# Decay masking, decay products and a convolution tap change engines in a two-layer hybrid trunk

## The chip, the cores and the metric

The kernel runs on one core of one Trainium2 chip. The metric is device time in microseconds (us) of one execution. Before the change the median of three runs is 2238.65 us, the lowest 2234.93 us and the highest 2241.45 us.

Engines are called PE (TensorE, matrix products), PEld (TensorE's weight loads), DVE (VectorE), ACT (ScalarE), POOL (GpSimd) and SP (SyncE, which issues most transfers).

## The reference, cut to what matters

Two layers of a transformer trunk over 512 latent tokens, with a context of 256 tokens before them; the width is 1024, everything is float32. Per layer, for context and latents with the same weights:

```
h   = rmsnorm(x) * (1 + scale) + shift
qkv, z, a, b, c_q, c_kv, k_rope = split(h @ w_in)
u   = silu(conv5(qkv))                     # short convolution over time, 5 taps, per column
q,k = l2norm(u_q), l2norm(u_k);  v = u_v
g   = -exp(a_log) * softplus(a + dt_bias); beta = sigmoid(b)
# gated delta rule in chunks of 64, in both directions of time, latents start from the context's state
gc    = cumsum(g)
decay = exp(where(i >= j, gc_i - gc_j, -inf))
A     = where(i > j, (k*beta) k^T * decay, 0);   solve (A + I) against v*beta and k*beta*exp(gc)
qk    = q k^T * decay;   qg = q * exp(gc)
scan over chunks: S, o
y   = concat(rmsnorm(o)*silu(z), latent_attention(...)) @ w_out
x  += gate1 * y;   x += gate2 * swiglu(modulated rmsnorm(x))
```

In the second layer the context is only needed for keys, values and the final state. At the end there is one rmsnorm.

## The kernel before, in words

All activations lie transposed, with 128 feature rows on the partitions and tokens along the free dimension. A large product is made of three products in a reduced float32 form: each operand is split into a high and a low part, `hi = copy(x)` on ACT and `lo = x - hi` on DVE (lines 205, 206, 210 to 212), and PE adds hi*hi, hi*lo and lo*hi (`gemm`, lines 214 to 222). Weights are split in the same way just ahead of their use, 512 columns at a time (`load_w`), so that PE, in its order, waits for ACT and DVE at each weight tile.

The work is written as generators, the streams: `ctx_in`, `ctx_mla`, `ctx_ffn`, `ctx_in1` once, and `ctx_chain`, `mod_rest`, `lat_in`, `lat_chain`, `mla_prep`, `mla_att`, `lat_ffn` for each layer (lines 1152 to 1313). After each step a stream yields three planned costs: how long the step takes until its successor can follow, the PE time and the DVE time in it. `weave` (lines 78 to 102) is the planner: it keeps a planned clock for PE and for DVE and a due time for each stream, and always writes out the next step of the stream that can start first on PE's planned clock; between equals the rank decides. The pair in `TUNE` (lines 51 to 70) is a stream's rank and a factor on its costs: a smaller factor brings a stream's steps closer together. Some steps wait for a name that another stream reports as done (`need`). The order of writing is a priority; the order on each engine can differ from it where an operand is late.

The delta rule's streams (`ctx_chain`, `lat_chain`) go through `gdn_pre` and `gdn_scan`. `gdn_pre` is run six times: for the context and for two halves of the latents' heads in layer 0, for the context and the two halves in layer 1. It works on tiles of 128 partitions by 16 units of 64 columns (128x1024). For each direction d it takes the broadcast cumulated decay `gb[d]`, which comes by a transfer on POOL's queue; if queries are wanted (five of six times) ACT writes `qg[d] = exp(gb[d])` (line 516); POOL masks `gb[d]` in place, in two halves of 64 partitions, with `affine_select` and the fill -1e30 (lines 517 to 520); DVE subtracts a column (line 523), and ACT takes exp (line 524). Then PE makes k k^T and q k^T and DVE multiplies them by the decay (lines 540 to 551). POOL multiplies `qg[d]` by q (line 555), fills four tiles (lines 558 to 561), and DVE solves the triangular systems in 31 steps of two small operations (lines 571 to 576). PE, ACT and DVE finish with products of 64x64 blocks. `gdn_scan` goes over the chunks in order of time.

`conv` (lines 433 to 443) takes a projected chunk in PSUM: POOL clears two columns at each edge of `raw`, ACT copies the chunk into its middle, DVE makes tap 0 as a product with a scalar (line 440) and adds taps 1 to 4 (line 442), and `silu2` ends it. A latent chunk is 128x512, a context chunk 128x256. There are 24 latent chunks (12 per layer) and 20 context chunks (12 and 8).

Of the kernel before, what the change touches and what calls it, by code (L numbers as in the profile page):

```python
# [14 lines left out]
AF = mybir.ActivationFunctionType  # L15
ALU = mybir.AluOpType
# [4 lines left out]
P = 128  # L21
# [11 lines left out]
SLOT = 776  # L33

C_ID, C_BLK1, C_TRIF, C_TRIB, C_SEL, C_MSK, C_ONE, C_BLKM, C_QB = 0, 128, 256, 384, 512, 520, 524, 525, 527
NCONST = 529
B_MOD, N1, N2, CW, AL, DT, GN, QN, KN, FN = 0, 48, 56, 64, 124, 132, 140, 141, 143, 144
NSMALL = 152

# [9 lines left out]


TUNE = {
    ("ctx_in", 0): (3, 0.749),
    ("ctx_mla", 0): (3, 0.7),
    ("ctx_ffn", 0): (3, 1.003),
    ("ctx_in1", 0): (2, 1.0),
    ("ctx_chain", 0): (0, 1.0),
    ("mod_rest", 0): (1, 0.7),
    ("lat_in", 0): (2, 0.595),
    ("lat_chain", 0): (1, 1.0),
    ("mla_prep", 0): (4, 1.064),  # L60
    ("mla_att", 0): (5, 0.374),
    ("lat_ffn", 0): (6, 1.0),
    ("ctx_chain", 1): (2, 0.85),
    ("mod_rest", 1): (1, 1.0),
    ("lat_in", 1): (1, 1.0),
    ("lat_chain", 1): (0, 0.6),
    ("mla_prep", 1): (5, 1.755),
    ("mla_att", 1): (5, 1.07),
# [37 lines left out]
def trunk_kernel(ctx, tc, xin, cc, wmod, small, win, wuq, wuk, wuv, wout, wgu, wdn, cst, rope, out):  # L106
    nc = tc.nc
    V, A, G, PE = nc.vector, nc.scalar, nc.gpsimd, nc.tensor
# [18 lines left out]
    def slot(tag, dt=F32, w=None):  # L127
        width = WIDTH[tag]
        t = sp.tile([P, width], dt, name=nm(tag), tag=tag, bufs=BUFS[tag])
        return t[:, 0:w or width]  # L130
# [4 lines left out]
    def sm(shape, tag, dt=F32, bufs=1):  # L135
        return mp.tile(shape, dt, name=nm(tag), tag=tag, bufs=bufs)

    def tt(out, a, b, op=ALU.mult, e=None):
        (e or V).tensor_tensor(out=out, in0=a, in1=b, op=op)  # L139

    def ts(out, a, s1, s2=None, op0=ALU.mult, op1=ALU.add, e=None):
        if s2 is None:
            (e or V).tensor_scalar(out=out, in0=a, scalar1=s1, scalar2=None, op0=op0)
        else:
            (e or V).tensor_scalar(out=out, in0=a, scalar1=s1, scalar2=s2, op0=op0, op1=op1)

    def stt(out, a, s, b, op0, op1):
        V.scalar_tensor_tensor(out=out, in0=a, scalar=s, in1=b, op0=op0, op1=op1)  # L148

    def act(out, a, f, **kw):  # L150
        A.activation(out, a, f, **kw)  # L151

    def cpy(out, a):
        act(out, a, AF.Copy)
# [4 lines left out]
    nc.sync.dma_start(out=cct, in_=cc)  # L159
    cst_t = cp.tile([P, NCONST], F32, name="cst")  # L160
    nc.sync.dma_start(out=cst_t, in_=cst)
# [267 lines left out]
    def silu2(dst, src, th):  # L429
        act(th, src, AF.Tanh, scale=0.5)  # L430
        stt(dst, th, 1.0, src, ADD, MUL)

    def conv(l, st, p, chunk, dst):
        n = st.n
        raw = slot(st.t, w=n + 4)
        G.memset(raw[:, 0:2], 0.0)
        G.memset(raw[:, n + 2:n + 4], 0.0)
        cpy(raw[:, 2:n + 2], p)
        cw = smalls[l][:, CW + 5 * chunk:CW + 5 * chunk + 5]
        ts(dst, raw[:, 0:n], cw[:, 0:1])  # L440
        for j in range(1, 5):
            stt(dst, raw[:, j:j + n], cw[:, j:j + 1], dst, MUL, ADD)
        silu2(dst, dst, raw[:, 0:n])

# [3 lines left out]
    def u3(t):  # L448
        return t.rearrange("p (c i) -> p c i", i=64)

    U = 16

    def gdn_pre(l, st, hjs, kf, qf, vf, gt, res):
# [6 lines left out]
        def col(t, d):  # L460
            return t[:, u0(d):u0(d) + U]

        full = qf is not None
        gb = [slot("g4") for _ in range(2)]
        kt = slot("g4")
        qg = [slot("g4") for _ in range(2)] if full else []
# [47 lines left out]
        for d in range(2):  # L514
            if full:
                act(qg[d], gb[d], AF.Exp)
            for hp in range(2):
                s = slice(64 * hp, 64 * hp + 64)
                G.affine_select(out=u3(gb[d])[s], in_=u3(gb[d])[s], compare_op=ALU.is_ge, fill=-1e30, base=0,
                                pattern=[[0, U], [1 if d == 0 else -1, 64]], channel_multiplier=-1 if d == 0 else 1)  # L520
            dc = sm([P, U], "dc")
            tt(dc, col(gcb, d), lw, ADD)
            tt(u3(gb[d]), u3(gb[d]), dc.unsqueeze(2).to_broadcast([P, U, 64]), SUB)
            act(gb[d], gb[d], AF.Exp)
            kw = sm([P, U], "kw", bufs=4)
            tt(kw, col(ekl, d), rw)
            kws.append(kw)
            yield 4, 0, 1.6
# [11 lines left out]
        for b in range(0, U, nb):  # L540
            pt = ps("B")
            pv = pt.rearrange("p (c z i) -> p c z i", z=nz, i=64)
            for c in range(nb):
                for z, f in enumerate((kf, qf)[0:nz]):
                    for hp in range(2):
                        s = slice(64 * hp, 64 * hp + 64)
# [5 lines left out]
            yield 3, 1, 1.6  # L552
        if qf is not None:
            for d in range(2):
                tt(qg[d], qf, qg[d], e=G)
        bm = gb
        bd, L, M = (slot("g4") for _ in range(3))
        G.memset(bd[:, 0:1], 0.0)
# [12 lines left out]
        for r in range(31):  # L571
            n, m = 31 - r, r + 1
# [39 lines left out]
        for dst, lh, rh in ((us, vv, (vs, vs)), (W, ke, vv)):  # L612
            for a in range(0, U, 4):
                pt = ps("B")
                pv = pt.rearrange("p (n d i) -> p n d i", d=2, i=64)
                for q in range(4):
                    n, hi = divmod(a + q, nh)
                    for d in range(2):
                        c = hi * nch + (nch - 1 - n if d else n)
                        for hp in range(2):  # L620
                            s = slice(64 * hp, 64 * hp + 64)
# [187 lines left out]
    scale = 96.0 ** -0.5  # L809
# [249 lines left out]
    class Mix:  # L1059
# [21 lines left out]
        def use(self, m, p):  # L1081
            l, st = self.l, self.st
            kind, hj = m
            if kind == "tail":
                ab = slot("m" if st is CTX else "ox", w=st.n)
                cpy(ab, p)
                self.kr = ab
                self.gates = gates(l, st, ab)
            elif kind in "kqv":
                g = [g for g in self.gset if hj in g][0]  # L1090
                f = self.f[g]
                i = g.index(hj)
                ch = {"q": 0, "k": 4, "v": 8}[kind] + hj
                if g in self.spilled:
                    if kind not in f:
                        f[kind] = dp.tile([len(g), P, st.n], F32, name=nm("fscr"), tag=nm("fscr"))
                    t = slot(st.t, w=st.n)
                    conv(l, st, p, ch, t)
                    nc.gpsimd.dma_start(out=f[kind][i], in_=t)
                else:  # L1100
                    if kind not in f:
                        f[kind] = slot("g4")
                    conv(l, st, p, ch, f[kind][:, st.n * i:st.n * i + st.n])
            elif kind == "z":
                self.z[hj] = self.part("z", hj)
                silu2(self.z[hj], p, slot(st.t, w=st.n))
            else:
                t = slot("m" if st is CTX else "hd", w=st.n)
                cpy(t, p)
                if kind == "ckv":  # L1110
                    self.ckv = t
                else:
                    self.cq.append(t)

        def stage(self, g):
            f = self.f[g]
            if g in self.spilled:
                for kind in "kqv":
                    t = slot("g4")
                    nc.sync.dma_start(out=t.rearrange("p (j t) -> p j t", j=len(g)), in_=f[kind].rearrange("j p t -> p j t"))  # L1120
                    f[kind] = t
            return gdn_pre(self.l, self.st, g, f["k"], f.get("q"), f["v"], self.gates, self.pre[g])
# [237 lines left out]
def _constants():  # L1360
    f = np.float32
    c = np.zeros((P, NCONST), f)
    p = np.arange(P)
    c[:, C_ID:C_ID + P] = np.eye(P, dtype=f)
    c[:, C_ONE] = 1.0 / D
    same = (p[:, None] // 64) == (p[None, :] // 64)
    c[:, C_BLKM] = (p < 64) / 64.0
    c[:, C_BLKM + 1] = (p >= 64) / 64.0
    c[:, C_BLK1:C_BLK1 + P] = same
    c[:, C_QB] = 64 * EPS * (p < 64)  # L1370
    c[:, C_QB + 1] = 64 * EPS * (p >= 64)
    c[:, C_TRIF:C_TRIF + P] = same & (p[:, None] <= p[None, :])
    c[:, C_TRIB:C_TRIB + P] = same & (p[:, None] >= p[None, :])
    for j in range(4):
        for r in range(2):
            c[32 * j + r, C_SEL + 2 * j + r] = 1.0
    first = (p // 32) % 2 == 0
    c[:, C_MSK] = first
    c[:, C_MSK + 1] = ~first
    c[:, C_MSK + 2] = -1.0 * first  # L1380
    c[:, C_MSK + 3] = -1.0 * ~first
    t = np.arange(NL)
    inv = f(10000.0) ** (-np.arange(0, 16, 2, dtype=f) / f(16))
    ang = []
    for pos in ((t // GRID_W).astype(f), (t % GRID_W).astype(f)):
        a = pos[:, None] * inv[None, :].astype(f)
        ang += [a, a]
    ang = np.concatenate(ang, axis=1).astype(f)
    sign = np.where((np.arange(32) % 16) < 8, -1.0, 1.0).astype(f)
    rope = np.concatenate([np.tile(np.cos(ang).T.astype(f), (4, 1)), np.tile(np.sin(ang).T * sign[:, None], (4, 1))], axis=1)  # L1390
    return c, rope
# [57 lines left out]
```

## Time and profile before

| | |
|---|---|
| median of 3 runs | 2238.65 us |
| the profiled execution: its time | 2228.82 us |
| its span, first to last instruction | 2227.0 us |
| PE busy | 2034.1 us, 91% |
| DVE busy | 1497.3 us, 67% |
| ACT busy | 871.5 us, 39% |
| POOL busy | 127.1 us, 6% |
| rate of all transfers in the first of 40 slices | 319 GB/s |
| mean granted clock of PE | 0.946 of full speed |

The busy time of an engine is the union of its instructions. PE's instructions are pipelined and their ends are modelled, so that a PE busy all the time can still be fed late. An idle time in brackets stands behind the instruction that ended it, with the engine and line that released it. In a row of stretches the numbers are the length, then each engine's busy time and (with an x) its instructions, PE's granted clock, the busy share of the transfer engines, and GB/s.

### The profile page before, as it was taken

To read this page: it belongs to the slowest core of one execution; us is meant where nothing else is said; L and a number is where in the kernel's file an instruction comes from. 1 tells how busy PE (TensorE), PEld (TensorE's weight loads), DVE (VectorE), ACT (ScalarE), POOL (GpSimd) and SP (SyncE) were. 2 spreads that over 40 slices of the span, in tenths; PEclk is the share of its full clock that TensorE was granted. 3 is DMA by queue.
4 is the path that set the end of the run, shared out by engine and by line. 5 is a ranking of instruction groups with operands and counts; after the bars stand their busy time and mean duration, and the time that the engine had idled before them with its cause. 6 is when DMAs were issued, how large, how long until landed. Compare 5 with 4: busy or idle time off the path is not lost. (4 is left out here: it accounts for less than half of the span.)

```text
span 2227.0 us, 40577 instructions
## 1 busy us (share of the span) xinstructions
PE 2034.1 (91%) x16048; PEld 1592.5 (72%) x16048; DVE 1497.3 (67%) x2926; ACT 871.5 (39%) x1541; POOL 127.1 (6%) x283
## 2 busy tenths in 40 slices
PE   5999988889898999899999998987876988999996
PEld 3776677889895567788888876765544667888885
DVE  4779678986678787778454458887787555444445
ACT  3335375543443434553323244444322234223233
POOL 0200013000201000100000000200200000000000
PEclk8999998899999999999999999997986999999998
DMA  8345613343445402343223245521110022233332
GB/s 319 135 147 180 194 43 119 124 158 120 119 130 161 142 11 92 98 141 97 81 78 98 95 141 199 163 73 34 38 34 11 30 76 75 95 97 97 95 99 76
DMA packets 130638, 240.42 MB, mean 108 GB/s; under 512 B 15184, under 2 KB 30064, under 8 KB 130448
## 3 DMA queue, kind: packets, MB, share of 16 engines
q1 hardware_dynamic: 124592, 224.10, 30.9%
q0 software_dynamic: 5856, 13.74, 2.2%
q8 instruction: 126, 2.06, 0.4%
q14 instruction: 64, 0.52, 0.1%
HBM read 228.24 MB, written 6.91 MB: 106 GB/s over the span
## 5 line engine op out<-in xcount | busy, mean ns | idle before, releaser
L221 PE MATMUL psA<-hx,wh 128*128 128x512 f32 x1680 | 535.0, 398 | 20.2 <-ACT hx L151 8.5
L151 ACT ACTIVATE wh<-wr 128x512 fp32r<-128x512 f32 (+2 forms) x410 | 249.2, 608 | 650.6 <-PE psA L221 480.3
L139 DVE TENSOR_TENSOR wl<-wr,wh 128x512 fp32r<-128x512 f32 (+2 forms) x410 | 270.6, 661 | 231.7 <-ACT wh L151 231.3
L221 PEld LDWEIGHTS psA<-hx,wh 128*128 128x128 f32 x1680 | 314.5, 190 | 107.6 <-issue 12.4
L221 PE MATMUL psA<-hx,wl 128*128 128x512 f32 x840 | 330.7, 394 | 5.3 <-DVE wl L139 5.3
L221 PE MATMUL psM<-hx,wh 128*128 128x512 f32 x704 | 217.6, 390 | 0.0
L221 PEld LDWEIGHTS psA<-hx,wl 128*128 128x128 f32 x840 | 159.0, 189 | 42.2 <-DVE wl L139 8.3
L151 ACT ACTIVATE fh<-fr 128x512 fp32r<-128x512 f32 (+3 forms) x186 | 110.9, 600 | 156.6 <-PE psM L221 44.1
L148 DVE SCALAR_TENSOR_TENSOR g<-psA,mod,g 128x512 f32<-128x512 f32 x112 | 83.9, 749 | 105.8 <-PE psA L221 105.6
L221 PEld LDWEIGHTS psM<-hx,wh 128*128 128x128 f32 x704 | 132.3, 188 | 27.2
L139 DVE TENSOR_TENSOR fl<-fr,fh 128x512 fp32r<-128x512 f32 (+3 forms) x186 | 120.5, 653 | 39.2 <-ACT fh L151 37.7
L221 PE MATMUL psM<-hx,wl 128*128 128x512 f32 x352 | 137.0, 389 | 0.0
L221 PE MATMUL psF<-m,fh 128*128 128x256 f32 x600 | 117.3, 294 | 6.5 <-ACT tc L151 5.0
L221 PE MATMUL psA<-hd,wh 128*128 128x512 f32 x384 | 120.4, 392 | 0.0
L221 PEld LDWEIGHTS psF<-m,fh 128*128 128x128 f32 x600 | 96.2, 195 | 13.0 <-ACT tc L151 6.6
L221 PE MATMUL psA<-ox,wh 128*128 128x512 f32 x320 | 100.7, 393 | 0.0
L221 PE MATMUL psF<-m,fl 128*128 128x256 f32 x300 | 86.8, 289 | 4.4 <-DVE fl L139 4.2
L226 PE MATMUL psA<-m,g 128*128 128x256 f32 x320 | 75.8, 398 | 8.6 <-DMA g<-win 3.9
L221 PEld LDWEIGHTS psA<-hd,wh 128*128 128x128 f32 x384 | 71.7, 188 | 16.4 <-DVE hd L139 1.1
L221 PE MATMUL psM<-m,fh 128*128 128x256 f32 x416 | 81.3, 293 | 1.6 <-ACT m L151 0.9
L226 PEld LDWEIGHTS psA<-m,g 128*128 128x128 f32 x320 | 63.0, 199 | 19.6 <-ACT m L151 7.6
L221 PEld LDWEIGHTS psM<-hx,wl 128*128 128x128 f32 x352 | 66.1, 188 | 13.6
(382 smaller groups left out, 3704.0 us busy)
## 6 DMA issues: line engine op xcount, KB each, us to landing
wr<-wgu SPq DMA_DIRECT2D x176, 256.0 KB, 2.6
m<-wmod SPq DMA_DIRECT2D x160, 256.0 KB, 4.3
fr<-wgu SPq DMA_DIRECT2D x88, 256.0 KB, 2.8
wr<-win SPq DMA_DIRECT2D x80, 256.0 KB, 3.3
wr<-wdn SPq DMA_DIRECT2D x64, 256.0 KB, 2.6
g<-win SPq DMA_DIRECT2D x20, 512.0 KB, 7.2
g<-wmod SPq DMA_DIRECT2D x16, 512.0 KB, 10.2
fr<-wdn SPq DMA_DIRECT2D x32, 256.0 KB, 2.7
```

The source lines that it names most:

```text
L139: (e or V).tensor_tensor(out=out, in0=a, in1=b, op=op)
L148: V.scalar_tensor_tensor(out=out, in0=a, scalar=s, in1=b, op0=op0, op1=op1)
L151: A.activation(out, a, f, **kw)
L221: PE.matmul(o, ww[:, wk], xx if n is None else xx[:, a:a + n], start=cnt == 0, stop=cnt == 3 * nk - 1)
L226: PE.matmul(o, w[:, k * P:k * P + P], x_, start=k == 0, stop=k == len(xs) - 1)
```

## The change

Three edits and new factors. The masking of `gb[d]` becomes one DVE minimum with a constant of 64 columns that is broadcast over the 16 units (3e38 where the element is kept, -1e30 elsewhere); the constant adds 128 columns to the tile `cst`, which is loaded at the start. The two products `qg[d] * q` go from POOL to DVE. In `conv` the centre tap becomes a second ACT copy out of PSUM with a scale per partition, which writes `dst` first; the four others are added on DVE as before. Eight factors of `TUNE` change; no rank does.

```diff
-NCONST = 529
+C_MIN = 529
+NCONST = 657
-    ("ctx_in", 0): (3, 0.749),
-    ("ctx_mla", 0): (3, 0.7),
-    ("ctx_ffn", 0): (3, 1.003),
+    ("ctx_in", 0): (3, 0.876),
+    ("ctx_mla", 0): (3, 0.595),
+    ("ctx_ffn", 0): (3, 0.702),
-    ("ctx_chain", 0): (0, 1.0),
+    ("ctx_chain", 0): (0, 0.7),
-    ("lat_in", 0): (2, 0.595),
+    ("lat_in", 0): (2, 0.416),
-    ("mla_prep", 0): (4, 1.064),
-    ("mla_att", 0): (5, 0.374),
+    ("mla_prep", 0): (4, 1.245),
+    ("mla_att", 0): (5, 0.4),
-    ("lat_in", 1): (1, 1.0),
+    ("lat_in", 1): (1, 0.7),
...
         cw = smalls[l][:, CW + 5 * chunk:CW + 5 * chunk + 5]
-        ts(dst, raw[:, 0:n], cw[:, 0:1])
-        for j in range(1, 5):
+        act(dst, p, AF.Copy, scale=cw[:, 2:3])
+        for j in (0, 1, 3, 4):
             stt(dst, raw[:, j:j + n], cw[:, j:j + 1], dst, MUL, ADD)
...
-            for hp in range(2):
-                s = slice(64 * hp, 64 * hp + 64)
-                G.affine_select(out=u3(gb[d])[s], in_=u3(gb[d])[s], compare_op=ALU.is_ge, fill=-1e30, base=0,
-                                pattern=[[0, U], [1 if d == 0 else -1, 64]], channel_multiplier=-1 if d == 0 else 1)
+            low = cst_t[:, C_MIN + 64 * d:C_MIN + 64 * d + 64]
+            tt(u3(gb[d]), u3(gb[d]), low.unsqueeze(1).to_broadcast([P, U, 64]), ALU.min)
...
-                tt(qg[d], qf, qg[d], e=G)
+                tt(qg[d], qf, qg[d])
...
+    i = np.arange(64)
+    for d, keep in enumerate((i[None, :] >= p[:, None] % 64, i[None, :] <= p[:, None] % 64)):
+        c[:, C_MIN + 64 * d:C_MIN + 64 * d + 64] = np.where(keep, 3e38, -1e30)
```

## Rows read from the trace of the kernel before

**Rows 1.** The page: busy time, share of the span, instructions.

```profile
PE 2034.1 (91%) x16048; PEld 1592.5 (72%) x16048; DVE 1497.3 (67%) x2926; ACT 871.5 (39%) x1541; POOL 127.1 (6%) x283
```

**Rows 2.** Stretches: latent projection of layer 0, tail of layer 1, last FFN.

```profile
150.00:250.00 100.00, 96.11 (x545) 70.70 (x545) 94.31 (x196) 42.86 (x74) 6.09 (x25) 0.98 0.52 172
1430.00:1785.00 355.00, 289.94 (x3209) 195.31 (x3207) 266.77 (x552) 118.56 (x203) 22.30 (x36) 0.84 0.14 42
1850.00:2190.00 340.00, 340.00 (x1497) 280.19 (x1496) 155.84 (x236) 104.79 (x173) 0.00 (x0) 1.00 0.30 96
```

**Rows 3.** Groups of instructions by line: busy us, mean ns, idle before.

```profile
L519 POOL TENSOR_SCALAR_AFFINE_SELECT g<-g 64x1024 f32<-64x1024 f32 x24 | 30.1, 1255 | 24.8 <-ACT g L151 22.7 <-DMA g<-gscr 1.3
L139 POOL TENSOR_TENSOR g<-g,g 128x1024 f32<-128x1024 f32 x10 | 27.2, 2723 | 0.7
L139 DVE TENSOR_TENSOR g<-g,dc 128x1024 f32<-128x1024 f32 x12 | 14.7, 1221 | 0.3
L139 DVE TENSOR_TENSOR g<-g,st 128x31 f32<-128x31 f32 (+15 forms) x186 | 63.2, 340 | 3.4
L143 DVE TENSOR_SCALAR g<-t,small 128x512 f32<-128x512 f32 x18 | 9.1, 504 | 3.5 <-ACT t L151 3.4
L143 DVE TENSOR_SCALAR g<-tc,small 128x256 f32<-128x256 f32 x20 | 7.0, 352 | 5.5 <-ACT tc L151 4.5 <-POOL g L469 0.4
L151 ACT ACTIVATE t<-psA 128x512 f32<-128x512 f32 x76 | 44.1, 581 | 4.3 <-PE psA L221 4.3
```

**Rows 4.** Order of time beside POOL's products in layer 1: start, length, what.

```profile
1593.73 0.16 DVE L139 TENSOR_TENSOR ro1t<-ro1t,oq 128x8 f32<-128x8 f32 x1
1595.08 2.34 DVE L139 TENSOR_TENSOR ro1t<-ro1y 128x8 f32<-128x8 f32 x1
1600.32 2.30 DVE L139 TENSOR_TENSOR ro1t<-ro1t,oq 128x8 f32<-128x8 f32 x1
...
1595.04 2.36 POOL L139 TENSOR_TENSOR g<-g,g 128x1024 f32<-128x1024 f32 x1
...
1602.87 1.98 PE L724 MATMUL psC<-cst,ro1y 128*64 128x128 f32 x16 [5.85 <-DVE ro1y L148]
```

**Rows 5.** Stretches at POOL's bursts and behind them.

```profile
94.00:107.00 13.00, 9.53 (x98) 7.94 (x97) 7.71 (x5) 7.41 (x11) 10.26 (x6) 1.00 0.31 98
...
352.00:366.00 14.00, 9.59 (x91) 8.05 (x92) 13.85 (x22) 4.88 (x7) 12.69 (x11) 0.54 0.29 95
366.00:380.00 14.00, 13.07 (x88) 10.98 (x85) 10.56 (x26) 9.54 (x23) 0.04 (x1) 0.73 0.36 128
...
590.00:603.00 13.00, 8.21 (x89) 7.18 (x87) 12.28 (x13) 5.48 (x10) 11.15 (x10) 0.84 0.27 78
603.00:620.00 17.00, 16.18 (x154) 15.77 (x155) 13.97 (x35) 9.05 (x14) 0.53 (x1) 0.82 0.41 133
...
1595.00:1605.00 10.00, 3.83 (x52) 3.32 (x52) 7.82 (x11) 1.95 (x3) 7.40 (x5) 0.69 0.01 2
1605.00:1615.00 10.00, 6.64 (x76) 4.00 (x75) 6.60 (x15) 6.34 (x9) 0.00 (x0) 0.79 0.09 27
```

**Rows 6.** Order of time at two other bursts.

```profile
102.50 5.65 DVE L148 SCALAR_TENSOR_TENSOR t<-g,al,t 128x512 f32<-128x512 f32 x3
109.40 0.74 DVE L148 SCALAR_TENSOR_TENSOR t<-g,al,t 128x512 f32<-128x512 f32 x1
...
105.81 8.86 PE L226 MATMUL psA<-m,g 128*128 128x256 f32 x32 [3.47 <-ACT m L151]
...
600.24 0.58 PE L221 MATMUL psM<-hd,fh 128*128 128x256 f32 x1 [3.84 <-DVE hd L139]
```

**Rows 7.** Layer 0: end of the second scan and of attention; one stretch.

```profile
828.50 1.04 PE L724 MATMUL psC<-cst,ro1y 128*64 128x128 f32 x16
...
845.15 1.03 PE L232 MATMUL psA<-acc,cst 128*64 128x512 f32 x4
...
406.00:416.00 10.00, 6.08 (x23) 4.34 (x22) 9.16 (x23) 5.80 (x11) 0.00 (x0) 0.75 0.15 53
```

## The prediction

> **What bounds the kernel now.** The page comes first: PE is busy 91% of the span and no other engine over 67% [rows 1], so the kernel is as fast as PE is fed, and a change is worth what it takes out of PE's idle time or gives back of its clock. Then the stretches: in the last FFN PE is busy all the time at the full clock, 2.4 GHz, while DVE needs under half of it [rows 2]; nothing in this change can help there. The stages with the delta rule are where time can move. During layer 0's latent projection DVE is busy 94% and PE 96%, two engines nearly level; in layer 1's tail PE stands still for 65 us of 355 at a granted clock of 0.84 [rows 2]. The third view is the order of time at the places that the change touches, where the reader is to see that POOL's operations stop DVE. A product of 8 columns takes DVE 0.16 us, but 2.34 and 2.30 us when it starts beside POOL's products of 2.36 us [rows 4] and 2.72 us in the mean [rows 3], and PE then waits 5.85 us for the result [rows 4]. DVE's busy share hides this: held instructions count as busy.
>
> **The change part by part.**
>
> *POOL's masks and products go.* There are 24 masks, 30.1 us, and 10 products, 27.2 us [rows 3]; together 57.3 us in six bursts, one per run of the decay part. In their place DVE gets 12 minima and 10 products of 128x1024. Neither is in the trace; the nearest row is DVE's subtraction of the same shape, also with a broadcast operand, 1.221 us [rows 3], and I take it for both: 22 x 1.221 = 26.9 us, 4.9 us in each of five bursts and 2.4 in the sixth. What DVE gets back is the time that it was held. Its bounds are 0, if every hold falls where DVE would have idled, and 57.3 us. The rows give a value between: in one burst two held products lose 4.3 us (2.34 + 2.30 less 2 x 0.16) to 5.1 us of POOL's products [rows 3, 4]; in another three modulating operations take 5.65 us [rows 6], while the same operation takes 0.74 a little later [rows 6], 2.2 for three. Operations that read PSUM and one tile are not seen to stretch. I take some 5 to 6 us per full burst: DVE's sum there comes out level, between -30 and +27 us over the whole kernel, -3 us taken.
>
> The gain is then in where the time lies. Before, a hold hits whatever stands at DVE's head, small operations on PE's path too; after, the 1.2 us operations take their place in the order. So I price PE's idle time burst by burst. At 94 to 107 us PE idles 3.5 us [rows 5], 3.47 of it behind ACT, which waits for those three held operations [rows 6]: 3 us come back. At 352 to 366 it idles 4.4 us, DVE busy 13.85 of 14 [rows 5]; the new operations fill the same queue: 1 us. At 590 to 603 it idles 4.8 us [rows 5], 3.84 of them behind one held `hd` split [rows 6]: 4 us. The burst near 940 has masks only, and at the one near 1408 PE is fed: nothing for both. At 1595 to 1605 it idles 6.2 us [rows 5], 5.85 in the one wait [rows 4]: 5 us. Sum 13 us, bounds 0 and the 18.9 us of idle time in the four bursts.
>
> *The clock.* Behind or in these bursts the granted clock falls, to 0.54 and 0.73, 0.84 and 0.82, 0.69 and 0.79 [rows 5], that is, part of each stretch ran at 1.2 GHz after PE had stood still. Busy time times the missing share bounds what a full clock would save: 0.46 x 9.59 + 0.27 x 13.07 + 0.16 x 8.21 + 0.18 x 16.18 + 0.31 x 3.83 + 0.21 x 6.64 = 14.7 us. Other idle times stand near each fall, so I take a third, 5 us; bounds 0 and 14.7.
>
> The Trainium skill has a rule for this, in SBUF — State Buffer, section "SBUF: two separate sides": GpSimd and a DVE operation with two SBUF inputs share a pair of ports as a lock that one of them holds for its whole instruction. The 2.34 us for 8 columns agrees. By that rule alone all of POOL's time is a hold wherever such an operation heads DVE's queue, and the bound of 57.3 us would be the value, for a return to DVE of some 30 us; by the rows, in which PSUM readers pass, it is about half. What the larger return would make of the time is rival 1.
>
> *The centre tap.* DVE loses one scalar product per chunk: 24 x 0.504 + 7.0 = 19.1 us [rows 3]. ACT gains one copy out of PSUM per chunk, at most 44 x 0.581 = 25.6 us [rows 3], with 871 us in a span of 2227 used [rows 1]. PE's bank comes free 0.58 us later, with a second bank in hand and 24 products between uses: hidden; if the cover were gone, 44 x 0.58 = 25.6 us. The first sum on DVE now waits for ACT's second copy, but the four sums in a row are DVE's load, not its start. What DVE saves matters where it is level with PE, the 12 chunks at 116 to 250 us [rows 2]: 6 us of DVE, of which PE's 3.9 idle us in 150 to 250 bound the use; I take 3. In layer 1's projection it is cover for the new operations, elsewhere nothing. Bounds 0 and 6.
>
> *The constant* is 64 KB more in the first transfers: 0.2 us at the 319 GB/s of the page's first slice.
>
> *The order.* By the planner's rule with the yielded costs, layer 1 keeps its order but for one exchange of steps. In layer 0, 30 instead of 21 of the context's solve steps stand ahead of the last latent projection; the first attention preparation moves up beside the context's output projection, so that the context's second modulation loses that filler; and the second scan ends 7 instead of 21 attention steps before the last. The first relieves the stretch after 250 us and loads DVE where the centre tap unloads it (nine pairs of operations of 0.34 us in the mean [rows 3], 6.1 us against 6). The second hits a stretch that is already thin, PE 6.08 of 10 us at clock 0.75 [rows 7]. The third uses cover that exists: the scan's last products end at 829.5 us and attention runs to 846.2, 16.6 us for its last 18 steps, of which 14 are 13 [rows 7]. Transfers keep their streams' order, and on SP's queue only steps of different streams swap. I take 0, bounds -15 and +15.
>
> Sum: 13 + 5 + 3 = 21 us. From the profiled execution's 2228.8 us that gives 2208; the three runs' median is 9.8 us above that execution, so from the median 2217.6, 2217 as forecast.
>
> **The rivals.**
>
> 1. *The hold costs more than I count.* PE's idle time in all four bursts goes, 18.9, with the 3.4 us behind the last one (10 less 6.64 busy [rows 5]), all of the clock, 14.7, and the tap's 6: 43 us, 2196. For it: the chain behind each burst also ends sooner, and layer 1's tail has 65 idle us [rows 2]. Against: other waits stand behind these.
> 2. *The order eats it.* The modulation near 406 us loses its filler: PE's 6.08 us of work [rows 7] leave, and as much again runs at half clock behind it: +12 us and a few more for the scan's late end, net about -6: 2233. For it: the row; against: moved work still fills another place.
> 3. *DVE is the worse for it (the other side).* If holds return nothing, because DVE has slack behind each, DVE gains 26.9 - 19.1 = 7.8 us, and the 4.9 us of new work per burst stands ahead of the splits that PE waits for, in the bursts at 352 and 590 where DVE is over 94% busy [rows 5]. Price: from 7.8 us up to 26.9; I take 10, 2249. It decides from the point where less than 7.8 us is returned. Against it speak the 4.3 us from one burst.
> 4. *The change does not do what it says*: the scheduler puts the new DVE operations so late that the decay chain waits for them and everything else cancels: 2238.
>
> **How the numbers follow.** Forecast 0.48 (its own range 2205 to 2229), rival 1 0.20, rival 2 0.13, rival 3 0.14, rival 4 0.05. About 0.3%, 6.7 us, is what a measurement of this kernel can tell from no change. Faster by that means under 2232: forecast, rival 1 and a third of rival 2, 0.72; rival 4 and the rest of rival 2 are the same, with a small part of rival 3, 0.16; slower 0.12. The range from 2187 to 2246 takes in rival 1 with its order bound and leaves out the worse part of rival 3.
>
> **What would show it.** POOL has no operation of 128x1024 but the fills; no 8-column operation of DVE over 0.3 us near the decay part; the minimum at 1.2 us; PE's waits of 5.85 and 3.84 us gone; DVE's busy time lower by some 20 us, ACT's higher by 20 to 25; PE's idle sum down from 193 us by 13 to 20 and the mean clock over 0.946. It would be wrong if the minima run at 2 us or more, if PE waits for DVE at the same places as long as before, or if layer 0 ends later than 850 us although its bursts are clean.

## The result and the profile after

| | before | after |
|---|---|---|
| median, same chip | 2239.14 us (2234.93 to 2241.45, 4 runs) | 2223.4 us (2222.33 to 2224.78, 4 runs) |
| ratio after to before, 95% interval | | 0.9932 [0.9915, 0.9949] |
| profiled execution: time, span | 2228.82, 2227.0 us | 2224.78, 2223.0 us |
| PE idle in that span | 192.9 us | 190.8 us |
| mean granted clock | 0.946 | 0.946 |

The change makes the kernel 15.7 us faster (0.7%); 21 were forecast. The two profiled executions show only 4 us of it, because the one of before was 10 us faster than its median. A second profile of the unchanged kernel (below) has a span of 2249.2 us. So a difference of ten microseconds between two single profiles means nothing here. What follows rests on ratios of many runs, on stretches that come out alike in several kernels, and on single waits.

In the kernel after, a line beyond 60 has a number higher by one (L139 is L140, L148 is L149). The page's first part of the kernel after, engine by engine: busy us, share, instructions. It answers to [rows 1].

```profile
PE 2032.2 (91%) x16048; PEld 1591.7 (72%) x16048; DVE 1474.6 (66%) x2904; ACT 889.5 (40%) x1583; POOL 69.6 (3%) x249
```

DVE lost 22.7 us, ACT gained 18, POOL lost 57.5; PE is as busy as before. The groups of new instructions, from the groups by line of the kernel after (busy us, mean ns, idle before), answer to [rows 3].

```profile
L140 DVE TENSOR_TENSOR g<-g,cst 128x1024 f32<-128x1024 f32 x12 | 14.6, 1220 | 10.7 <-ACT g L152 7.1 <-DMA g<-gscr 3.6
L140 DVE TENSOR_TENSOR g<-g,g 128x1024 f32<-128x1024 f32 x10 | 12.2, 1216 | 0.0
L152 ACT ACTIVATE g<-psA,small 128x512 f32<-128x512 f32 (+1 forms) x30 | 17.8, 594 | 0.0
L152 ACT ACTIVATE t<-psA,small 128x512 f32<-128x512 f32 x6 | 4.1, 683 | 5.8 <-DMA fscr<-t 5.8
L152 ACT ACTIVATE g<-psF,small 128x256 f32<-128x256 f32 x8 | 3.7, 466 | 0.0
```

The first two are the minimum and the decay product, 26.8 us together, the last three the centre tap, 25.6 us: both as forecast. The stretches of the kernel after that answer to [rows 5]: length, busy us (instructions) of PE, PEld, DVE, ACT and POOL, granted clock, transfer share, GB/s.

```profile
94.00:107.00 13.00, 12.94 (x111) 10.30 (x110) 8.33 (x12) 10.32 (x16) 1.02 (x2) 1.00 0.47 139
352.00:366.00 14.00, 8.10 (x62) 6.83 (x61) 13.49 (x25) 6.79 (x15) 2.77 (x6) 0.76 0.24 62
366.00:380.00 14.00, 12.56 (x94) 10.35 (x94) 9.85 (x20) 6.94 (x18) 0.00 (x0) 0.75 0.17 49
590.00:603.00 13.00, 12.34 (x200) 11.88 (x197) 8.19 (x22) 5.62 (x12) 3.34 (x9) 1.00 0.65 168
603.00:620.00 17.00, 16.86 (x181) 15.69 (x180) 15.16 (x34) 11.22 (x20) 0.50 (x1) 1.00 0.35 113
1595.00:1605.00 10.00, 9.45 (x93) 5.92 (x93) 8.76 (x23) 6.71 (x11) 0.00 (x0) 1.00 0.34 89
1605.00:1615.00 10.00, 4.08 (x85) 3.14 (x82) 7.92 (x21) 5.11 (x6) 0.00 (x0) 0.85 0.09 26
```

At 94, 590, 603 and 1595 us PE's idle time is nearly gone (0.1, 0.7, 0.1 and 0.6 us, against 3.5, 4.8, 0.8 and 6.2) and the clock is full. At 352 PE idles 5.9 us, 1.5 more than before. But these are the same times, not the same work: in the kernel after, the minima and products of three of these bursts stand at 344 to 365, at 601 to 618 and at 1600 to 1617 us. The last burst can be read by its work instead. Between the two rows shown next, kernel before and then kernel after (PE in order of time), lie the same 169 PE instructions:

```profile
1590.39 0.45 PE L483 MATMUL psB<-cst,g 64*64 64x64 f32 x8
...
1616.35 1.65 PE L961 MATMUL psB<-hx,hx 128*128 128x512 f32 x3 [4.71 <-DVE g L139]
```

```profile
1596.33 0.45 PE L484 MATMUL psB<-cst,g 64*64 64x64 f32 x8
...
1614.74 1.65 PE L960 MATMUL psB<-hx,hx 128*128 128x512 f32 x3 [5.92 <-DVE g L140]
```

They take 26.0 us before and 18.4 after, so this burst gave back 7.5 us. The idle 5.9 us of the stretch from 1605 are the wait of the second row. Before, it was there too, with 4.7 us, and reached beyond the stretch of [rows 5], so that 1.2 us of it is new.

In that burst the small operations run at their own length again. DVE in order of time, kernel after (start, length, what), against 2.34 and 2.30 us in [rows 4]:

```profile
1597.92 0.16 DVE L140 TENSOR_TENSOR ro1t<-ro1y 128x8 f32<-128x8 f32 x1
...
1599.67 0.15 DVE L140 TENSOR_TENSOR ro1t<-ro1t,oq 128x8 f32<-128x8 f32 x1
1599.74 1.22 DVE L140 TENSOR_TENSOR g<-g,cst 128x1024 f32<-128x1024 f32 x1
...
1600.95 0.16 DVE L149 SCALAR_TENSOR_TENSOR ro1y<-ro1t,ro1y 128x8 f32<-128x8 f32 x1
```

One operation of 8 columns is still held in the kernel after, beside one of the six fills of 128x1024 that stay on POOL. It ends when the fill ends:

```profile
595.65 1.01 POOL L559 MEMSET g<- 128x1024 f32 x1
...
596.04 0.65 DVE L146 TENSOR_SCALAR ro1y<-oq 128x8 int32<-128x8 int32 x1
```

### The profile page after: what moved, and what is told of

It reads as the page before. It is cut to its first block, busy times and chain, and to the rows that moved or that the text cites. A ratio compares the mean times of both kernels' runs of the same rounds, so it can differ in the third digit from the quotient of the medians.

```text
span 2223.0 us, 40501 instructions
## 1 busy us (share of the span) xinstructions
PE 2032.2 (91%) x16048; PEld 1591.7 (72%) x16048; DVE 1474.6 (66%) x2904; ACT 889.5 (40%) x1583; POOL 69.6 (3%) x249
## 4 chain that ended last, share of the span: by engine, by line
PE 76%; DVE 10%; DMA 6%; ACT 5%; issue 3%; SPq 0%; POOL 0%; ACTq 0%; DVEq 0%; POOLq 0%
PE psA L222 35%; PE psM L222 14%; PE psF L222 4%; PE psB L960 3%; PE psA L233 2%; PE psA L227 2%; PE psB L621 2%; PE psM L233 2%; PE psC L668 1%; DVE fl L140 1%; DMA m<-wmod 1%; ACT t L152 1%; DVE g L140 1%; PE psC L680 1%; PE psC L691 1%
## 5 line engine op out<-in xcount | busy, mean ns | idle before, releaser
L140 DVE TENSOR_TENSOR wl<-wr,wh 128x512 fp32r<-128x512 f32 (+2 forms) x410 | 269.5, 658 | 229.0 <-ACT wh L152 228.4
L149 DVE SCALAR_TENSOR_TENSOR g<-psA,mod,g 128x512 f32<-128x512 f32 x112 | 83.9, 749 | 104.9 <-PE psA L222 104.6
L222 PEld LDWEIGHTS psM<-hx,wh 128*128 128x128 f32 x704 | 132.2, 188 | 27.2
L140 DVE TENSOR_TENSOR fl<-fr,fh 128x512 fp32r<-128x512 f32 (+3 forms) x186 | 120.0, 648 | 43.3 <-ACT fh L152 39.9
```

The source lines that it names most:

```text
L222: PE.matmul(o, ww[:, wk], xx if n is None else xx[:, a:a + n], start=cnt == 0, stop=cnt == 3 * nk - 1)
```

## The experiments

The theory: the whole gain comes from POOL's products and masks, which hold DVE and through it PE; the tap and the factors bring nothing or little. The rivals: the tap brings part of it (through DVE's load in the projection), the new order brings or eats part, or POOL's time costs nothing beyond the moments in which PE visibly waited. All ratios are to the kernel before on the same chip, with 95% intervals.

**1. e1_nopool: masks and products on DVE alone**, the tap and the factors as before.

```
-                G.affine_select(out=u3(gb[d])[s], ...)          # two halves, POOL
+            tt(u3(gb[d]), u3(gb[d]), low...to_broadcast(...), ALU.min)
-                tt(qg[d], qf, qg[d], e=G)
+                tt(qg[d], qf, qg[d])
```

> The kernel before with the masks and the decay products on DVE; the convolution and the planner's factors are the old ones. If POOL's hold on DVE is what the change removes, this edit alone brings most of the gain: 10 to 18 us, 2221 to 2229 us, with the 8-column operations beside the decay part back at 0.17 us and PE's wait of 5.85 us near 1600 gone. If DVE is the worse for the added work (rival 3), 2242 to 2249 us with DVE over 95% busy at the bursts. If the factors or the tap made the gain, within 3 us of 2239.

Measured: 2220.22 us, 0.9915 [0.9899, 0.9931]. This part alone brings 19 us, one more than the range expected for it, and at least as much as the whole change.

**2. e2_tap: the tap on ACT alone.**

```
-        ts(dst, raw[:, 0:n], cw[:, 0:1])
-        for j in range(1, 5):
+        act(dst, p, AF.Copy, scale=cw[:, 2:3])
+        for j in (0, 1, 3, 4):
```

> The kernel before with the centre tap on ACT and nothing else. Forecast: 3 us less, 2233 to 2239 us, DVE busy 19 us lower and ACT busy 22 to 25 us higher. If the tap carries the gain, 2224 to 2229 us; if the second copy out of PSUM holds PE's banks, slower than 2242 us with longer waits of PE for ACT in the projections.

Measured: 2252.33 us, 1.0063 [1.0043, 1.0084]. Slower by 14 us: the tap's term had the wrong sign. DVE's busy time fell by 11 us (1485.9), ACT's rose by 19 (890.5).

**3. e3_order: the eight factors alone.**

```
-    ("lat_in", 0): (2, 0.595),  ("mla_prep", 0): (4, 1.064),  ...
+    ("lat_in", 0): (2, 0.416),  ("mla_prep", 0): (4, 1.245),  ...   # all eight
```

> The kernel before with the eight new factors and nothing else. In the changed kernel's trace layer 0 ends 8 us later than in the trace before, though POOL's bursts are gone, and layer 1, whose order hardly changes, takes 12 us less. If that is the order's doing (rival 2), this kernel is 5 to 12 us slower: 2244 to 2251 us, all of it in layer 0. If the order is neutral, 2236 to 2242 us. If the order needs the other edits to pay, it may lose here and not in the whole.

Measured: 2255.34 us, 1.0070 [1.0051, 1.0088]. Slower by 16 us, at the edge of the bounds of -15 and +15.

**4. e4_three: the change with the old factors** (e1 and the tap). Its diff is that of e1 and e2 together.

> The changed kernel with the old factors: masks, products and tap moved, old order. If the order eats part of the gain (rival 2), this is the fastest: 2211 to 2218 us, below the changed kernel's 2223. If the order is neutral, 2220 to 2226 us. If the new order is what makes room for the moved work, slower than the changed kernel: 2227 to 2234 us.

Measured: 2230.67 us, 0.9959 [0.9943, 0.9975]. Against e1 the tap costs 0.44%, 10 us.

**5. a0_before: the kernel before, unchanged**, for a second profile of it.

> The kernel before, unchanged, as a second profile of it and as a measure of how far two runs of one program lie apart. Expected 2236 to 2244 us, a ratio of 1 within 0.3%. The profile shown ahead of the prediction took 2228.8 us, 10 us under the median; if this one ends layer 0 some 10 us after 1317.7 us, the difference between the profile before and the median lies in layer 0.

Measured: 2243.2 us, 0.9999 [0.9984, 1.0015]. The profile shows how much two executions of one program differ. The end of layer 0 is marked by the first transfer of `xscr` on POOL's queue. In order of time on POOL, kernel before:

```profile
1317.70 0.57 POOL L261 DMA_DIRECT2D xscr<-g  x1 [355.59 <-DVE g L148]
```

In the second profile the same row stands at 1334.57 us, 16.9 us later. The rest of the span, layer 1, is 909.3 us in the one and 914.6 in the other. So layer 1 can be read from single profiles to some 5 us, layer 0 cannot.

**6. e7_notap: the change with the old tap** (e1 and the new factors).

> The changed kernel with the old convolution (tap 0 on DVE): masks and products on DVE, new factors. The tap alone cost 14 us and cost 10 us on top of the moved masks and products, so if the tap itself is slow wherever it stands, this is the fastest yet: 2208 to 2217 us. If the new factors were made for the tap (they load DVE where the tap unloads it), it is slower than the changed kernel: 2226 to 2238 us.

Measured: 2235.19 us, 0.9961 [0.9945, 0.9976]. On e1 the factors cost 0.46%, 10 us.

**7. e8_dummy: e1 with ten POOL products that nothing waits for.** They read finished tiles, two per decay part with queries, and write a tile that nobody reads; the order on PE, DVE, ACT and SP is that of e1.

```
+            for d in range(2):
+                tt(idle_t, qf, kt, e=G)
```

> The kernel with masks and products on DVE (old tap, old factors), and beside them ten POOL products of 128x1024 per run of the whole kernel into a tile that nobody reads, two per decay part with queries; nothing waits for them, and the other engines' orders are unchanged. Theory of the hold: POOL's 27 us hold DVE for some 20 of them, 8-column products of 2 us appear again, and the kernel loses 6 to 14 us against the 2220 us of the kernel without them: 2226 to 2234 us. Rival: POOL's work only mattered through what waited for its results (masks late, products late): then no change, 2217 to 2223 us, though POOL is 27 us busier.

Measured: 2239.08 us, 0.9985 [0.997, 1.0], against 0.9915 and 0.9913 for e1: 0.7% or 16 us, 9 to 23 by the ends of the intervals; 6 to 14 were expected. DVE is busy 1506.7 us against 1489.5 in e1, with the same 2948 instructions in the same order: 17 us of hold beside 27 us of POOL. The group of them on POOL, kernel e8 (busy us, mean ns):

```profile
L140 POOL TENSOR_TENSOR idle<-g,g 128x1024 f32<-128x1024 f32 x10 | 27.2, 2724 | 48.0 <-ACT g L152 35.0 <-issue 12.6
```

And one pair of them in order of time on POOL and DVE, and PE behind it, kernel e8:

```profile
1615.81 5.47 POOL L140 TENSOR_TENSOR idle<-g,g 128x1024 f32<-128x1024 f32 x2 [8.69 <-ACT g L152]
...
1613.90 0.16 DVE L149 SCALAR_TENSOR_TENSOR ro1y<-ro1t,ro1y 128x8 f32<-128x8 f32 x1
...
1616.53 2.35 DVE L149 SCALAR_TENSOR_TENSOR ro1y<-ro1t,ro1y 128x8 f32<-128x8 f32 x1
...
1619.40 1.90 DVE L140 TENSOR_TENSOR ro1t<-ro1y 128x8 f32<-128x8 f32 x1
...
1622.79 1.97 PE L725 MATMUL psC<-cst,ro1y 128*64 128x128 f32 x16 [3.36 <-DVE ro1y L149]
```

The same operation takes 0.16 us ahead of POOL's pair and 2.35 beside it, and PE waits 3.36 us for the result, the wait of [rows 4] come back. No wait in this trace ends on one of the idle products, and PE, DVE and ACT run the same instructions in the same order as in e1, so what costs is the hold. The Trainium skill states the rule, in SBUF — State Buffer, section "SBUF: two separate sides": a POOL operation, or a DVE operation with two SBUF inputs beside a POOL operation that reads SBUF, keeps the port pair that both use to itself until it ends. The trace agrees (2.35 against 0.16 us).

**8. e6_prod: only the products move to DVE**, the masks stay on POOL.

```
-                tt(qg[d], qf, qg[d], e=G)
+                tt(qg[d], qf, qg[d])
```

> The kernel before with the ten products on DVE and the masks still on POOL. The products held DVE 27 us and nothing on the path waits for them, so by the theory of the hold this is worth about half of the 19 us that masks and products gave together: 2226 to 2234 us. If the gain came from the masks' place on the decay chain, under 4 us: 2236 to 2243 us.

Measured: 2230.41 us, 0.9942 [0.9923, 0.9961]. The products carry 0.6%, 13 us, within the range expected; the masks are left with 0.3% of e1, though the two intervals overlap. The masks on POOL lengthened meanwhile. Groups on POOL, kernel e6, against 1255 ns in [rows 3]:

```profile
L519 POOL TENSOR_SCALAR_AFFINE_SELECT g<-g 64x1024 f32<-64x1024 f32 x24 | 39.4, 1642 | 26.9 <-ACT g L151 24.2 <-DMA g<-gscr 1.7
```

The long ones are held by DVE. Here one starts just behind a DVE product and ends 1.00 us after it, having taken 2.19 us; the shortest take 1.14:

```profile
92.96 1.23 DVE L139 TENSOR_TENSOR g<-g,g 128x1024 f32<-128x1024 f32 x1
...
93.00 2.19 POOL L519 TENSOR_SCALAR_AFFINE_SELECT g<-g 64x1024 f32<-64x1024 f32 x1 [1.22 <-ACT g L151]
```

**9. e9_copy: e1 with the tap's copy added and not used.** DVE keeps its tap 0, so no work is new but ACT's copy and the longer use of the PSUM bank. The order is new too: from 51 to 56 us on, the traces of e1 and e9 differ in the order on PE, DVE and ACT, since the order on each engine is set with the copy in it.

```
+        act(spare_t[:, 0:n], p, AF.Copy, scale=cw[:, 2:3])
         ts(dst, raw[:, 0:n], cw[:, 0:1])
```

> The kernel with masks and products on DVE, old tap and old factors (0.9915 of before), and in each convolution one more ACT copy out of PSUM into a tile that nobody reads: the tap's load on ACT without what it takes from DVE. If the tap loses in layer 0 because the second copy holds ACT and PE's banks, this loses the same 10 us or more: 2229 to 2236 us. If ACT's copy is hidden, within 4 us of 2220, and the tap's loss comes from DVE's order or the schedule.

Measured: 2229.23 us, 0.9951 [0.9933, 0.997], 0.38% or 8 us above e1. Adding the copy costs what the tap costs, by its time on ACT, by its use of the bank or by the order that comes with it; that DVE is busy 13 us less in e4 than in e1 (1476.3 against 1489.5) brings nothing that can be seen.

Where it costs most: in the context's and latents' projections of layer 0. The stretch from 50 to 265 us holds them. Kernel e1, then e9, then e4:

```profile
50.00:265.00 215.00, 210.59 (x1224) 159.74 (x1223) 175.04 (x387) 88.47 (x167) 11.51 (x64) 0.99 0.53 174
```

```profile
50.00:265.00 215.00, 206.69 (x1186) 156.84 (x1186) 173.65 (x380) 98.25 (x187) 11.57 (x64) 0.98 0.51 167
```

```profile
50.00:265.00 215.00, 205.32 (x1185) 155.16 (x1184) 165.71 (x354) 98.32 (x187) 11.40 (x64) 0.99 0.50 167
```

ACT is 10 us busier in both, PE 4 to 5 us idler, though in e4 DVE has 9 us less to do. The stage ends 6.3 us later: the first clearing of the context's attention on POOL stands at 265.1 us in e1 and at 271.5 and 271.4 in e9 and e4. One wait can be named. PE in order of time in the context's projection, kernel e1, then e9:

```profile
51.69 4.58 PE L227 MATMUL psA<-m,g 128*128 128x256 f32 x20 [0.47 <-ACT tc L152]
```

```profile
53.26 3.69 PE L228 MATMUL psA<-m,g 128*128 128x256 f32 x16 [2.21 <-DMA g<-win]
```

Without the copy PE waits 0.47 us there, for ACT to empty the bank, in all nine profiles. With it PE waits 2.2 to 3.1 us, for input weights by the trace, in all five (e2, e4, e9 and both profiles of the kernel after). The weights don't come later: the fifth tile of them lands at 53.7 us in e1 and at 53.1 in e9. What differs is PE's order. In the nine profiles without the copy the first PE instruction with this tile is the 65th of the projection, in the five with it the 49th, so PE stands until the tile is there. ACT at that place, kernel e9: its second copy of the bank stands behind a tanh of the chunk before.

```profile
51.09 0.39 ACT L152 ACTIVATE tc<-psA 128x256 f32<-128x256 f32 x1 [1.84 <-PE psA L228]
51.63 0.42 ACT L152 ACTIVATE tc<-g 128x256 f32<-128x256 f32 x1 [0.16 <-DVE m L144]
51.95 0.46 ACT L152 ACTIVATE spare<-psA,small 128x256 f32<-128x256 f32 x1
```

So the bank is read until 52.41 us, 0.9 us after the first copy ended at 51.48. That can explain up to 0.9 of the 1.7 us of longer waiting. The rest is PE's order, since the tile comes only at 53.1. In the whole stretch this is all that PE is seen to wait for a second copy to leave its bank (kernel e9; total, times, longest):

```profile
PE psA L223 <- ACT spare L152: 0.3, 1, 0.3
```

The other 2 us are spread over short waits, whose cause the runs don't separate. In layer 1 the copy costs nothing that can be seen (894.5 us in e9, 895.5 and 897.6 in two profiles of e1).

**10. e10_nudge: e1 with two factors moved by 1 to 2%**, so that 257 of PE's 8933 rows change places, about as many as between e1 and e4 (277), by the count in its expectation.

```
-    ("lat_in", 0): (2, 0.595),  ("mla_prep", 0): (4, 1.064),
+    ("lat_in", 0): (2, 0.605),  ("mla_prep", 0): (4, 1.075),
```

> The same base (masks and products on DVE, old tap), with two factors of layer 0 moved by 1% (lat_in 0.595 to 0.605, mla_prep 1.064 to 1.075): 257 of 8933 of PE's rows change place, as many as the tap moves (277), with no work added or taken. If layer 0's loss by the tap is an accident of the order, this too moves by several us either way, 2210 to 2232, all of it before the end of layer 0; if an order that differs by this little is worth nothing, 2217 to 2223 us.

Measured: 2219.39 us, 0.9912 [0.9891, 0.9933], as e1. So this change of order costs nothing. But in the traces it begins only at 700 us, and the copy's begins at 51 us, in the projections where the tap loses. Whether an order that differs there costs the 8 to 10 us without a copy was not tried.

**11 and 12. e11_again and e12_after: e1 and the kernel after once more, side by side on one chip.** No edit.

> The kernel with masks and products on DVE, old tap and old factors, once more, beside the changed kernel on one chip: which of the two is faster. First measurement 0.9915 of before against 0.9932, intervals that overlap. Expected 2216 to 2224 us, the same as the changed kernel within 0.3%; layer 1's part of the span 897 us in both.

> The changed kernel once more, beside the previous kernel on one chip. Expected 2220 to 2228 us; if the tap and the new factors together are worth something, below the previous kernel by more than 4 us, if they cost, above it by as much.

Measured: 2221.15 us, 0.9913 [0.9893, 0.9933], and 2230.77 us, 0.9948 [0.9932, 0.9964]. Masks and products on DVE with the old tap and the old factors is the fastest version of the study, with e10 level: 0.35% or 8 us under the kernel after on this chip, with intervals that just touch, and 6 us if the two ratios of each are averaged (0.9914 against 0.9940).

Layer 1 from all profiles, span less the first `xscr` row, tells the parts apart without layer 0's noise:

| POOL does | kernels | layer 1, us |
|---|---|---|
| masks and products | before, a0, e2, e3 | 909.3, 914.6, 906.8, 910.8 |
| idle products | e8 | 907.8 |
| masks | e6 | 901.8 |
| neither | e1, e11, e10, e9, e4, e7, after, e12 | 897.6, 895.5, 895.6, 894.5, 897.0, 897.6, 897.0, 896.7 |

Eight profiles with and without the tap's copy, with old and new factors, lie within 3.1 us of each other, 13 to 14 us in the mean below the four with POOL's work. Layer 1's gain is POOL's alone.

PE's idle time, the span less PE's busy time, is steadier than the span and sorts the versions: 192.9 and 196.5 us in the two profiles of before, 183.9, 183.9 and 184.0 with masks and products on DVE (e1, e11, e10), 194.9 with the idle products back (e8), 185.7 with the products alone on DVE (e6), and 190.4 to 191.3 wherever the copy, the factors or both are added (e9, e4, e7, after, e12). Tap and factors on the kernel before give 202.0 and 211.4.

Not all of the gain is at places where PE was seen to wait for a held result. The burst near 1408 us, costed at nothing because PE is fed, is followed by short waits for weight splits on DVE and ACT. PE in order of time there, kernel before:

```profile
1420.53 0.50 PE L221 MATMUL psA<-hx,wl 128*128 128x512 f32 x1 [0.87 <-DVE wl L139]
1424.65 0.73 PE L221 MATMUL psA<-hx,wh 128*128 128x512 f32 x2 [0.49 <-ACT wh L151]
1429.43 0.50 PE L221 MATMUL psA<-hx,wl 128*128 128x512 f32 x1 [1.00 <-DVE wl L139]
```

2.4 us in sum. The stretch of the kernel after that answers to it (its layer 1 starts 8 us later) has no idle time of PE:

```profile
1389.00:1439.00 50.00, 50.00 (x343) 36.81 (x342) 42.45 (x70) 30.77 (x50) 4.25 (x27) 1.00 0.60 183
```

For the factors the stretches of layer 0 show where they cost; these too are the same times and not the same work. Kernel e1, then the kernel after:

```profile
300.00:400.00 100.00, 90.86 (x1125) 79.53 (x1120) 80.04 (x178) 57.08 (x113) 11.19 (x28) 0.91 0.36 105
400.00:500.00 100.00, 82.08 (x655) 77.67 (x654) 86.13 (x193) 44.70 (x81) 0.00 (x0) 0.86 0.41 123
700.00:800.00 100.00, 90.92 (x1114) 52.29 (x1112) 73.96 (x138) 37.34 (x68) 3.92 (x8) 0.91 0.39 120
```

```profile
300.00:400.00 100.00, 83.44 (x946) 71.49 (x944) 83.55 (x186) 51.61 (x106) 10.87 (x25) 0.90 0.32 92
400.00:500.00 100.00, 84.78 (x848) 79.75 (x846) 81.14 (x182) 47.68 (x88) 0.00 (x0) 0.90 0.42 131
700.00:800.00 100.00, 84.86 (x884) 49.37 (x876) 76.38 (x138) 40.20 (x73) 3.90 (x8) 0.91 0.33 104
```

From 700 to 800 us PE is busy 83.7 to 86.0 us in the four profiles with the new factors (after, e12, e7, e3) and 88.8 to 93.8 in the ten with the old ones; from 300 to 400 it is 82.8 to 85.3 against 87.0 to 90.9. Between 400 and 500 some 3 us come back against e1.

## Why the prediction was right, point by point

**POOL's hold and the clock** (13 + 5 = 18 us forecast). Measured 19 us (e1). The mechanism was right and so, nearly, were both terms: PE's idle time is 9 to 13 us lower in e1, e11 and e10 than in the two profiles of before, against 13 taken. The mean granted clock of all runs on e1's chip is 0.943 against 0.940; an estimate from these, 0.003 of some 2040 us of PE's work, is 6 us against 5 taken. The sharing out was lucky. The sum had 8 us of the idle time in layer 0 and 5 in layer 1. Measured, layer 1 idles 7 to 10 us less, and layer 0 between 6 less and 1 more. In layer 1 the burst at 1595 gave 7.5 us, clock included, and that at 1408, priced at nothing, another 2.4: before, DVE was late with weight splits up to 20 us behind the burst. The ten products alone cost 16 us when put back without a reader, so the hold also costs where the rows showed no wait, as rival 1 said; but its sum of 37 us for POOL and clock is far from the 19. The bounds of 1.221 us per new operation held to 5 ns.

Two readings of [rows 6] were inexact. Of the three modulating operations in 5.65 us two were held and the third took its 0.74, and ACT waited for the first alone. And the wait of 3.84 us stood behind more than the `hd` split, which took 1.30 us: three operations of 32x256 ahead of it on DVE took 1.04 to 1.56 us, while such an operation takes 0.28 a little later. Neither changes a price.

**DVE's time level** (-3 taken for holds and new operations, -19.1 for the tap). The sum of -22.1 met the measured -22.7 by luck: without the tap DVE's busy time falls by 7.8 us (e1), so about 34.6 us of held time came back and not 30, and the tap then took 14.9 (after against e1) and not 19.1.

**The centre tap** (3 us gain, bounds 0 and 6). This step failed. The price was laid out, 0.58 us of ACT and of the bank per chunk and 25.6 us in all if the cover were gone, and then taken as hidden because a second bank stood ready. Measured: a loss of 10 us on e1 and of 14 alone, and of 8 for the bare copy, with 6.6 us more idle time of PE, 4 of it in the projections of layer 0. What the sum left out is that a new instruction on ACT also changes the order on PE. Bank and order together make the one wait that can be named 1.7 us longer, the bank at most 0.9 of it; the rest stays open. And DVE's 94% there was read as a limit: 9 us less of it brought PE nothing.

**The constant** (0.2 us): nothing contradicts it; not measured alone.

**The order** (0, bounds -15 and +15). As a single edit it costs 16 us, on e1 10 us, on e4, where the tap is in, nothing or a gain of up to some 6 (0.9959 to 0.9948 and 0.9932, intervals that overlap). So 0 stands for this change, but not for the reason given: PE loses time at the two places that rival 2 named, before 400 us and, some 6 us, from 700 to 800, ahead of the scan's late end, of which the prediction said that it uses cover that exists. That these are rival 2's causes is argued from the place alone. Rival 2's arithmetic, 12 us and a few, was right for the factors alone. Why tap and factors together cost no more than either alone stays open; that the factors were suited to a projection with ACT's copy in it would explain it, and e7 came out as that expects, but no run shows the cause.

The sum with measured terms: 19 for POOL, less 10 for the tap, give e4's 9 us, and 3 to 6 more with the factors are the 12 to 16 us of the two comparisons. The forecast of 2217 came near by a gain in the tap that didn't exist and an order term that happened to be small.

**What was to be seen.** Right: POOL's 128x1024 operations but the fills are gone, the minimum takes 1.22 us, PE's waits of 5.85, 3.84 and 3.47 us are gone (a wait of 3.8 us for `hd` near 1685 us is in both lists), DVE's busy time is 23 us lower. 8-column operations are at 0.16 us but for the one of 0.65 beside a fill. Short: ACT +18 instead of 20 to 25. Wrong: PE's idle time fell by 2 us instead of 13 to 20 and the clock stayed at 0.946. Part of that is the fast profile of before, and the tap and the order took some 7 us of idle time back. The mark of 850 us for layer 0 tells nothing: attention ends at 851.2 us in the profile after, but at 859.5 in the second profile of the unchanged kernel, and at 852.1 in e11, one of the fastest kernels.

Rival 3, a worse DVE, is refuted by e1. Rival 4 is refuted by the groups and by the ratio.

## What to carry to other kernels

POOL work between two SBUF tiles is not free because nobody waits for it: look in DVE's order of time for a tiny operation with a length of microseconds, and price POOL's time by what PE waits behind such operations, in full length if DVE is the feeder. Before adding work to an engine that is 40% busy in the mean, expect that it also moves the order on the other engines: compare in the trace, stage by stage, what PE asks for next with when it is there. A control run with another order has to differ in that same stage. And factors of a planner belong to one set of edits: try the edits with the old ones too, as here the part without tap and factors was the fastest.

## What the runs showed of the hardware that was not expected

POOL products of 27.2 us that nobody reads cost the kernel 16 us, over half of their own length, with the instruction order on the other engines unchanged. The mask halves on POOL took 1642 ns instead of 1255 once the products had gone to DVE, the held ones behind a DVE product, so the hold goes both ways. DVE operations with one input in SBUF were held too: 8 columns took 0.65 us beside a fill of POOL in the kernel after. A scaled copy out of PSUM took ACT 680 ns for 128x512, a plain one 582 (kernel e9), and 465 against 382 for 128x256. Two executions of the unchanged program had spans of 2227.0 and 2249.2 us, and 16.9 of those 22.2 us lay in layer 0.
